# A hybrid mixer block: conditioning products one unit behind their loads, more taps in the xBC stage, one matmul for the context's high and low parts, pairwise squares at the front

## The chip, the cores and the metric

The kernel runs on one core of one Trainium2 chip. The metric is device time in microseconds of one execution, and lower is better.

## What is computed

One layer of a diffusion backbone over 512 latent tokens, with 256 context tokens as a prefix; the model width is 1024 and everything is fp32. Cut to what matters:

```python
mod_lat = split(silu(c) @ w_ada + b_ada, 6)         # conditioning: 6 x 1024 values for the latents
mod_ctx = split(silu(c_ctx) @ w_ada + b_ada, 6)     # of these the context needs the first two
h_ctx = modulate(rms_norm(ctx, norm1_g), mod_ctx[0], mod_ctx[1])
_, ctx_states = token_mixer(h_ctx, ...)             # the final SSD states of the context alone
h = modulate(rms_norm(x, norm1_g), mod_lat[0], mod_lat[1])

# token_mixer
z, xbc, dt, cv_in, pool_in, gate_logits = split(h @ w_in)
xbc = silu(depthwise_conv(xbc, 5 taps))             # latents and context
y = ssd_bidirectional(xbc, dt, ...)                 # chunked scans, both directions
y_ssd = rms_norm(y * silu(z)) @ ssd_w_out
y_conv = silu(layer_norm(depthwise_conv(a * sigmoid(b), 31 taps))) @ cv_w_out
y_pool = pool_mixer(pool_in)
merged = g0 * y_ssd + g1 * y_conv + g2 * y_pool     # sigmoid gates
x = x + mod_lat[2] * (merged @ w_out)

h = modulate(rms_norm(x, norm2_g), mod_lat[3], mod_lat[4])
x = x + mod_lat[5] * swiglu(h)
return rms_norm(x, final_g)
```

## The kernel before

Activations lie with 128 channels on the partitions and the tokens along the free axis: the 1024 channels of the latents are eight tiles of 128 x 512. A weight unit is 128 output channels by all inputs, 128 x 1024 values or 512 KB. To keep fp32 accuracy each operand is split into a high part, rounded to the format that TensorE takes in one pass, and a low part, the remainder. A product is then three matmuls into one PSUM bank (`mm3`, lines 132 to 137): high by high, high weight by low activation, low weight by high activation. `load_unit` (116) loads a unit into a raw buffer (`load_raw`, 111, three buffers named `wr`), ScalarE casts it to the high part `whi` (121) and VectorE subtracts to get the low part `wlo` (123). The context's activations `hc` are split the same way; the high and low part of one tile lie side by side, 256 columns each.

**Order of the work.** Instructions are written in program order; a planner then gives each engine a fixed order, by priorities and its own costs, and hands out the buffers of a name as they come free. `tc.high_priority` and `later(n)` move work forward and back in that order. `Ordered` (56) wraps the engines up to line 339: there each engine keeps the order of the source. Each engine, and the transfer queue of SyncE, then takes its work strictly in its fixed order.

**Front (176 to 338).** The first 2048 columns of the conditioning weights come in eight loads of 1 MB (`ada_load`), alternating with the tiles of x and the first three units of the input projection. `ada_mm(i)` multiplies one of them (16 small matmuls) and has ScalarE copy the result, `ada_out(i)` turns it onto the partitions with small matmuls, and VectorE adds the bias. An even i gives the scale of two channel tiles, the odd one behind it their shift. The mean square of x is an fp32 matmul with a matrix of 1/1024 (`mean`), which the trace shows as two matmuls; it reads `acc`, the sum of eight squares that ScalarE makes and VectorE adds (`sq_acc`). `rnorm` gives the reciprocal root. `h_scale` (VectorE) and `h_shift` (ScalarE and VectorE) make the high and low parts of the normalised input; `first(us, ks)` runs the matmuls of the units us for the tiles ks; `first_split` splits such a unit. `warm(n)` issues n matmuls whose result is not used. (In the trace all that goes through `Ordered` has line 62.)

**Input projection (350 to 741).** The convolution of 31 taps along rows (`conv31`) is 90 steps of two VectorE instructions each (line 403). `conv_steps(n)` releases n steps at a low priority; `CONV_STEPS_XBC` says how many in each of the twelve units of the xBC stage. In that stage (721 to 740) each unit is multiplied with the latents and, for the first ten, with the context; `conv5` runs five taps (669 on VectorE) and `xbc_tail` transposes on TensorE and builds the context's states.

**Scan, gates, convolution output (744 to 906).** The SSD scan of four chunks and two groups, woven with the units of z, of the two gates, and of the convolution output (`wcv`). What does not fit is written to HBM (`mrg`, `gat`, `zd`, `yd`).

**SSD output (927 to 942) and output projection (992 to 1025).** For each of eight tiles the SSD product is merged with `gat` and `mrg`, read back from HBM, and split; then the output projection `wout`, its first two tiles together, its last three in halves of the tokens.

**The other conditioning values.** The conditioning weights behind the first 2048 columns are 32 units, spread over the stages. `ada(n)` (854) loads n units of 512 KB into `wr` buffers and has VectorE multiply each with silu(c) and sum it along the free axis into one column of `mod_l` (line 861). It is called in `gate_tiles` (4 units), in the convolution output (4), in the SSD output (8), in the output projection (8) and in the down projection of the FFN (8).

**FFN (1028 to 1220).** Gate and up units, most of them by a scheme of seven half-size products (`fast_pair`), then the down projection.

Of the kernel before, what the change touches and what calls it, by code (L numbers as in the profile page):

```python
# [11 lines left out]
ALU = mybir.AluOpType  # L12
# [10 lines left out]
GATES_BEFORE_LN = 5  # L23
WOUT_HALVED = 3
CONV_STEPS_EARLY = (30, 18)
CONV_STEPS_XBC = (0, 0, 0, 1, 1, 1, 2, 2, 2, 2, 2, 2)
TAILS_KEPT_XBC = (1, 1, 1, 1, 1, 0, 0, 0, 0, 0, 0, 0)
I_CV, I_PL, I_XBC, I_Z, I_G1, I_G0 = 0, 12, 26, 38, 46, 54

# [23 lines left out]
def hybrid_block(ctx, tc, x, cx, cck, cc, wad, wada, vec, prm, cst, inv, win, wdt, wcv, wpl, wso, wout, wgu, wdn, out):  # L53
# [22 lines left out]
    def pt(pool, shape, tag, bufs, dt=F32):  # L76
        return pool.tile(shape, dt, tag=tag, name=nm(tag), bufs=bufs)
# [31 lines left out]
    lng_n, ssg_n, fin_n = neg[:, 0:6], neg[:, 6:14], neg[:, 14:22]  # L109

    def load_raw(src, n):
        raw = pt(per, [P, 1024], "wr", 3)
        nc.sync.dma_start(raw[:, :n], src)
        return raw

# [170 lines left out]
    ada_load(4)  # L286
    ada_out(0, sb)
    warm(14)
    acc = pt(per, [P, T], "sum", 1)
    for t in range(KT):  # L290
        sq_acc(acc, xs[t], t == 0, T)
    S.activation(junk, eps_t, AF.Abs_reciprocal_sqrt)
    first_split(0)
    sb = ada_mm(1)
    ada_load(5)
    first_load(2)
    ms = psp()
    PE.matmul(ms, mean, acc, start=True, stop=True)
    ada_out(1, sb)
    r = acc  # L300
    rnorm(ms, T, r)
    warm(4)
    h_scale(0, 1)
    sb = ada_mm(2)
    ada_load(6)
    ada_out(2, sb)
    h_shift(0, 1)
    warm(4)
    sb = ada_mm(3)
    ada_load(7)  # L310
    wdt_t = slot_c()[:, 0:256]
    nc.sync.dma_start(wdt_t, wdt)
    first((0,), (0, 1))
    h_scale(2, 3)
    ada_out(3, sb)
    first_split(1)
# [190 lines left out]
    def ctx_norm():  # L507
        x3 = xc[:, 0:2, :].rearrange("p a (t n) -> p (a t) n", n=TC)
        nc.sync.dma_start(x3, cx)
        xs_c = [x3[:, t, :] for t in range(KT)]  # L510
        r = norm_sum(xs_c, TC)
        hq = [slot_h([P, 4, 2, TC], F32R) for _ in range(2)]
        for t in range(KT):
            h = hq[t // 4][:, t % 4]
            make_h(xs_c[t], r, m1_c[:, t : t + 1], mod_c[:, t : t + 1], h[:, 0, :], h[:, 1, :])
            hc.append((h[:, 0, :], h[:, 1, :]))

    def pool_all():
        plp, waiting = [], []
# [201 lines left out]
    for q, i in enumerate((8, 9, 10, 11, 0, 1, 2, 3, 4, 5, 6, 7)):  # L721
        w = load_unit(win[I_XBC + q])
        o = mmp()
        for k in range(KT):
            mm3(o, w, k * P, hh[k], k == 0, k == KT - 1)
        pad = slot_c()
        nc.gpsimd.memset(pad[:, 0:2], 0.0)
        nc.gpsimd.memset(pad[:, 514:518], 0.0)
        S.copy(pad[:, 2:514], o)
        if i < 10:  # L730
            oc = mmp()
            for k in range(KT):
                mm3(oc[:, :TC], w, k * P, hc[k], k == 0, k == KT - 1)
            nc.gpsimd.memset(pad[:, 774:776], 0.0)
            S.copy(pad[:, 518:774], oc[:, :TC])
        conv_steps(CONV_STEPS_XBC[q], mark[-1])
        while len(tails) > TAILS_KEPT_XBC[q]:
            drain(tails.pop(0))
        tails.append(xbc_tail(i, pad))
        next(tails[-1], None)  # L740
# [110 lines left out]
    for i in range(24):  # L851
        adas.append(((2, 4, 3)[i // 8], i % 8))

    def ada(n=1):
        for _ in range(n):
            if not adas:
                return
            chunk, t = adas.popleft()
            raw = load_raw(wada[(chunk - 2) * 8 + t], 1024)
            i = chunk * 8 + t  # L860
            V.tensor_tensor_reduce(  # L861
                raw, raw, silb[0], 1.0, vc("b_ada", i), ALU.mult, ALU.add, mod_l[:, i : i + 1]
            )

    load_sil(f1.tile([P, 1024], F32, tag="sil1", name="sil1"))
    gens = [ssd_gen(0), ssd_gen(1)]
# [27 lines left out]
    with later(9000):  # L894
        for m in range(8):
            w = load_unit(wcv[m], 768)
            oc = mmp()
            for k in range(6):
                mm3(oc, w, k * P, cvy[k], k == 0, k == 5)
            sp = tmp()  # L900
            S.copy(sp, oc)
            nc.sync.dma_start(mrg[:, m, 1, :], sp)
            ada(m % 2)
    for z in range(4):
        for g in gens:
            next(g)
# [20 lines left out]
    for m in range(8):  # L927
        w = load_unit(wso[m])
        o = mmp()
        for k in range(KT):  # L930
            mm3(o, w, k * P, y_hl[k], k == 0, k == KT - 1)
        ga, mo = slot_a(), slot_c().rearrange("p (a b) -> p a b", b=T)
        nc.sync.dma_start(ga, gat[:, m])
        nc.sync.dma_start(mo, mrg[:, m])
        S.activation(ga, ga, AF.Sigmoid)
        V.tensor_tensor(mo[:, 1, :], mo[:, 1, :], ga[:, 1, :], ALU.mult)
        V.tensor_tensor(mo[:, 0, :], mo[:, 0, :], mo[:, 1, :], ALU.add)
        V.tensor_tensor(ga[:, 0, :], o, ga[:, 0, :], ALU.mult)
        V.tensor_tensor(mo[:, 0, :], mo[:, 0, :], ga[:, 0, :], ALU.add)
        mr = mo[:, 0, :]  # L940
        split(mg[m][0], mg[m][1], mr)
        ada(1)

    x1 = slot_x([P, KT, T])
    acc = pt(per, [P, T], "sum", 1)
# [72 lines left out]
    for sl in halves:  # L1018
        for m, (w, o) in zip(range(nh, 8), last):
            ms = rms_head(sl) if m == 7 else None  # L1020
            project(o, [(w, KT)], mg, sl)
            with tc.high_priority():
                residual(m, o, mod_l[:, 16 + m : 17 + m], xp[m // 2][:, m % 2, :], sl, slot_m(), ms)
            prescale(m, sl)
        h2_half(ms, sl)
    tc.keep_in_program_order(S.activation(junk, eps_t, AF.Silu))
    ph1.close()
# [171 lines left out]
    hid = hs  # L1199

    acc = pt(per, [P, T], "sum", 1)
    for m in range(8):
        ada(1)
        o = mmp()
# [129 lines left out]
```

## Time and profile before

| | |
|---|---|
| median of 3 runs | 977.23 us (976.6 to 978.72) |
| the profiled execution | 976.52 us, of it 974.7 us from its first to its last instruction |
| TensorE busy | 948.8 us (97%), 5420 matmuls |
| VectorE busy | 764.9 us (78%) |
| ScalarE busy | 492.2 us (50%) |
| transfers | 151.67 MB, mean 156 GB/s |
| granted TensorE clock, mean | 0.996 |

How to read it: the span is what the trace sees; the time is that of the whole execution. TensorE's matmuls overlap, so the duration of one is longer than the spacing between two. The granted clock is the share of TensorE's full clock that the chip allowed.

### The profile page before, as it was taken

What the parts mean: (1) busy time and instruction counts of PE and PEld (TensorE: products, weight loads), DVE (VectorE), ACT (ScalarE), POOL (GpSimd) and SP (SyncE); (2) the same over time, 40 slices, a digit from 0 to 9 for tenths busy, and PEclk for the clock granted to TensorE, in tenths of its full rate; (3) what the DMA queues carried; (4) which work ended last, traced back from release to release, by engine and by line L of the source; (5) the groups of instructions that cost most, each with busy time, mean ns of one, the idle gap of its engine ahead of it and who ended that gap; (6) DMA issues with size and microseconds to landing.
All of it is one profiled execution on the core that took longest, in us unless ns stands there. A gap on an engine that the chain in (4) does not pass through costs nothing.

```text
span 974.7 us, 14173 instructions
## 1 busy us (share of the span) xinstructions
PE 948.8 (97%) x5420; PEld 803.6 (82%) x5420; DVE 764.9 (78%) x1165; ACT 492.2 (50%) x815; POOL 15.9 (2%) x58
## 2 busy tenths in 40 slices
PE   6999999999999999999999989999999999999996
PEld 4678888888887776777888769989999999888885
DVE  5589999967889999987876976999889888643333
ACT  5683597335445254644844434745555556432331
POOL 0000000000000000000000000000000000000000
PEclk9999999999999999999999999999999999999998
DMA  9753455321112346665578984223232323343422
GB/s 364 282 187 110 164 179 173 109 87 65 67 65 76 108 162 195 216 205 196 176 259 318 363 278 170 91 104 131 101 117 87 119 99 122 127 141 109 136 79 87
DMA packets 55492, 151.67 MB, mean 156 GB/s; under 512 B 5760, under 2 KB 16512, under 8 KB 54272
## 3 DMA queue, kind: packets, MB, share of 16 engines
q1 hardware_dynamic: 55424, 150.77, 44.6%
q8 instruction: 42, 0.69, 0.3%
q14 instruction: 26, 0.21, 0.1%
HBM read 134.43 MB, written 16.32 MB: 155 GB/s over the span
## 4 chain that ended last, share of the span: by engine, by line
PE 86%; DVE 7%; DMA 4%; ACT 2%; issue 1%; SPq 0%; DVEq 0%; ACTq 0%
PE mm L137 19%; PE mm L135 19%; PE mm L136 19%; PE mm L1122 10%; PE ps L1122 8%; PE mm L62 1%; DMA C<-mrg 1%; DVE wlo L123 1%; DVE A L403 1%; PE ps L1039 1%; PE ps L763 1%; PE y L825 1%; PE ps L62 1%; PE ps L715 1%; DMA wr<-in_wso_dram 1%
## 5 line engine op out<-in xcount | busy, mean ns | idle before, releaser
L135 PE MATMUL mm<-hh,whi 128*128 128x512 f32 (+1 forms) x612 | 242.4, 396 | 0.0
L137 PE MATMUL mm<-hh,wlo 128*128 128x512 f32 (+1 forms) x612 | 241.2, 394 | 0.5 <-DVE wlo L123 0.5
L136 PE MATMUL mm<-hl,whi 128*128 128x512 f32 x576 | 228.9, 397 | 0.0
L121 ACT CAST whi<-wr 128x1024 fp32r<-128x1024 f32 (+1 forms) x115 | 116.9, 1019 | 212.1 <-PE mm L136 167.4
L123 DVE TENSOR_TENSOR wlo<-wr,whi 128x1024 fp32r<-128x1024 f32 (+1 forms) x112 | 132.2, 1183 | 63.1 <-ACT whi L121 62.0
L137 PEld LDWEIGHTS mm<-hh,wlo 128*128 128x128 f32 x612 | 115.0, 188 | 28.3 <-issue 2.8
L135 PEld LDWEIGHTS mm<-hh,whi 128*128 128x128 f32 x612 | 115.1, 188 | 26.0 <-issue 1.7
L136 PEld LDWEIGHTS mm<-hl,whi 128*128 128x128 f32 x576 | 108.3, 188 | 25.0 <-issue 2.7
L403 DVE SCALAR_TENSOR_TENSOR A<-U,vec_t,A 128x504 f32<-128x504 f32 (+14 forms) x180 | 115.4, 684 | 0.1
L129 ACT CAST shi<-S 128x1024 fp32r<-128x1024 f32 x36 | 37.9, 1052 | 32.1 <-DVE S L1110 26.3
L1122 PE MATMUL mm<-T,shi 128*128 128x256 f32 x288 | 53.5, 283 | 0.0
L669 DVE SCALAR_TENSOR_TENSOR C<-C,vec_t,C 128x772 f32<-128x772 f32 (+1 forms) x48 | 46.9, 977 | 4.9 <-ACT C L667 2.4
L130 DVE TENSOR_TENSOR slo<-S,shi 128x1024 fp32r<-128x1024 f32 x36 | 44.1, 1225 | 5.8 <-ACT shi L129 5.7
L818 ACT ACTIVATE E<-E,sbias 128x128 f32<-128x128 f32 x128 | 40.0, 392 | 10.6 <-DMA E<-cumd 10.5
L1122 PEld LDWEIGHTS mm<-T,shi 128*128 128x128 f32 x288 | 44.8, 191 | 0.0
L129 ACT CAST whi<-wr 128x1024 fp32r<-128x1024 f32 (+1 forms) x36 | 30.0, 835 | 26.0 <-PE ps L1122 21.4
L861 DVE CUSTOM_DVE_ANT_0 wr<-wr,sil,vec_t 128x1024 f32<-128x1024 f32 x24 | 30.8, 1282 | 13.4 <-DMA wr<-in_wada_dram 13.4
L137 PE MATMUL mm<-H,wlo 128*128 128x256 f32 (+1 forms) x124 | 38.0, 307 | 2.9 <-DVE wlo L123 2.8
L1122 PE MATMUL mm<-T,slo 128*128 128x256 f32 x144 | 40.8, 284 | 0.0
L130 DVE TENSOR_TENSOR wlo<-wr,whi 128x1024 fp32r<-128x1024 f32 (+1 forms) x36 | 34.5, 958 | 7.6 <-ACT whi L129 6.0
L135 PE MATMUL mm<-H,whi 128*128 128x256 f32 (+1 forms) x124 | 37.8, 305 | 0.0
L136 PE MATMUL mm<-H,whi 128*128 128x256 f32 (+1 forms) x124 | 37.7, 304 | 0.0
(383 smaller groups left out, 2039.4 us busy)
## 6 DMA issues: line engine op xcount, KB each, us to landing
wr<-in_win_dram SPq DMA_DIRECT2D x62, 512.0 KB, 3.7
wr<-in_wgu_dram SPq DMA_DIRECT2D x44, 512.0 KB, 3.4
wr<-in_wada_dram SPq DMA_DIRECT2D x32, 512.0 KB, 4.0
E<-cumd SPq DMA_DIRECT2D x16, 512.0 KB, 5.3
wr<-in_wdn_dram SPq DMA_DIRECT2D x16, 512.0 KB, 3.9
X<-in_wad_dram SPq DMA_DIRECT2D x4, 1024.0 KB, 10.6
H<-in_wad_dram SPq DMA_DIRECT2D x4, 1024.0 KB, 11.2
mrg<-tmp SPq DMA_DIRECT2D x16, 256.0 KB, 4.0
```

Source lines behind the costliest of these rows:

```text
L121: S.copy(hi[:, :n], raw[:, :n])
L123: V.tensor_tensor(lo[:, :n], raw[:, :n], hi[:, :n], ALU.subtract)
L129: S.copy(dst_hi, src)
L130: V.tensor_tensor(dst_lo, src, dst_hi, ALU.subtract)
L135: PE.matmul(o, hi[:, col : col + P], rh, start=first, stop=False)
L136: PE.matmul(o, hi[:, col : col + P], rl, start=False, stop=False)
L137: PE.matmul(o, lo[:, col : col + P], rh, start=False, stop=last)
L403: V.scalar_tensor_tensor(accs[e][:, :, o], ins[e][:, :, q], vc("dw_w", (2 * j + e) * 31 + 15 + d), accs[e][:, :, o], ALU.mult, ALU.add)
L669: tap = V.scalar_tensor_tensor(a[:, 0:n], pad[:, k : n + k], vc("conv_w", i * 5 + k), a[:, 0:n], ALU.mult, ALU.add)
L818: S.activation(dec[d][:, j, :], dec[d][:, j, :], AF.Identity, bias=sbias[:, z, c : c + 1])
L861: V.tensor_tensor_reduce(raw, raw, silb[0], 1.0, vc("b_ada", i), ALU.mult, ALU.add, mod_l[:, i : i + 1])
L1122: PE.matmul(o[:, left], x[:, cs], rhs[k][y], start=first and k + n == 0, stop=k == 3 and n == 2, skip_group_check=True,)
```

## The change

- *Front.* The eight squares are added in four pairs; the four sums go through the averaging matrix one after the other, into one PSUM bank, three ahead of `ada_mm(1)` and the last behind it. `h_shift(0, 1)` moves ahead of `ada_mm(2)`, one `warm(4)` goes, and `first((0,), (0, 1))` moves ahead of `ada_mm(3)`.
- *xBC.* `CONV_STEPS_XBC` grows from 15 steps to 24. The context's high weight part meets the high and low activation parts in one matmul of 512 columns, whose two halves VectorE adds afterwards.
- *Conditioning.* `ada` now loads a unit and multiplies the one loaded before it (`ada_product`, `ada_rest`). The convolution output takes 5 units in place of 4, the SSD output 7 in place of 8, and the down projection issues its first load ahead of its loop. There are four raw buffers in place of three.

```diff
--- before.py
+++ after.py
@@ -23,7 +23,7 @@
 GATES_BEFORE_LN = 5
 WOUT_HALVED = 3
 CONV_STEPS_EARLY = (30, 18)
-CONV_STEPS_XBC = (0, 0, 0, 1, 1, 1, 2, 2, 2, 2, 2, 2)
+CONV_STEPS_XBC = (1, 1, 1, 2, 2, 2, 3, 3, 3, 2, 2, 2)
 TAILS_KEPT_XBC = (1, 1, 1, 1, 1, 0, 0, 0, 0, 0, 0, 0)
 I_CV, I_PL, I_XBC, I_Z, I_G1, I_G0 = 0, 12, 26, 38, 46, 54
 
@@ -109,7 +109,7 @@
     lng_n, ssg_n, fin_n = neg[:, 0:6], neg[:, 6:14], neg[:, 14:22]
 
     def load_raw(src, n):
-        raw = pt(per, [P, 1024], "wr", 3)
+        raw = pt(per, [P, 1024], "wr", 4)
         nc.sync.dma_start(raw[:, :n], src)
         return raw
 
@@ -286,31 +286,37 @@
     ada_load(4)
     ada_out(0, sb)
     warm(14)
-    acc = pt(per, [P, T], "sum", 1)
+    sq = []
     for t in range(KT):
-        sq_acc(acc, xs[t], t == 0, T)
+        q = slot_c()[:, :T] if t % 2 == 0 else tmp()
+        S.activation(q, xs[t], AF.Square)
+        if t % 2:
+            V.tensor_tensor(sq[-1], sq[-1], q, ALU.add)
+        else:
+            sq.append(q)
     S.activation(junk, eps_t, AF.Abs_reciprocal_sqrt)
     first_split(0)
+    ms = psp()
+    for q in sq[:3]:
+        PE.matmul(ms, mean, q, start=q is sq[0], stop=False)
     sb = ada_mm(1)
+    PE.matmul(ms, mean, sq[3], start=False, stop=True)
     ada_load(5)
     first_load(2)
-    ms = psp()
-    PE.matmul(ms, mean, acc, start=True, stop=True)
     ada_out(1, sb)
-    r = acc
+    r = pt(per, [P, T], "sum", 1)
     rnorm(ms, T, r)
     warm(4)
     h_scale(0, 1)
+    h_shift(0, 1)
     sb = ada_mm(2)
     ada_load(6)
     ada_out(2, sb)
-    h_shift(0, 1)
-    warm(4)
+    first((0,), (0, 1))
     sb = ada_mm(3)
     ada_load(7)
     wdt_t = slot_c()[:, 0:256]
     nc.sync.dma_start(wdt_t, wdt)
-    first((0,), (0, 1))
     h_scale(2, 3)
     ada_out(3, sb)
     first_split(1)
@@ -513,7 +519,7 @@
         for t in range(KT):
             h = hq[t // 4][:, t % 4]
             make_h(xs_c[t], r, m1_c[:, t : t + 1], mod_c[:, t : t + 1], h[:, 0, :], h[:, 1, :])
-            hc.append((h[:, 0, :], h[:, 1, :]))
+            hc.append((h[:, 0, :], h.rearrange("p a n -> p (a n)")))
 
     def pool_all():
         plp, waiting = [], []
@@ -730,9 +736,12 @@
         if i < 10:
             oc = mmp()
             for k in range(KT):
-                mm3(oc[:, :TC], w, k * P, hc[k], k == 0, k == KT - 1)
+                ks = slice(k * P, k * P + P)
+                PE.matmul(oc, w[0][:, ks], hc[k][1], start=k == 0, stop=False, skip_group_check=True)
+                PE.matmul(oc[:, :TC], w[1][:, ks], hc[k][0], start=False, stop=k == KT - 1, skip_group_check=True)
             nc.gpsimd.memset(pad[:, 774:776], 0.0)
             S.copy(pad[:, 518:774], oc[:, :TC])
+            V.tensor_tensor(pad[:, 518:774], oc[:, TC:], pad[:, 518:774], ALU.add)
         conv_steps(CONV_STEPS_XBC[q], mark[-1])
         while len(tails) > TAILS_KEPT_XBC[q]:
             drain(tails.pop(0))
@@ -851,16 +860,24 @@
     for i in range(24):
         adas.append(((2, 4, 3)[i // 8], i % 8))
 
+    loaded = deque()
+
+    def ada_product():
+        i, raw = loaded.popleft()
+        V.tensor_tensor_reduce(raw, raw, silb[0], 1.0, vc("b_ada", i), ALU.mult, ALU.add, mod_l[:, i : i + 1])
+
     def ada(n=1):
         for _ in range(n):
-            if not adas:
-                return
-            chunk, t = adas.popleft()
-            raw = load_raw(wada[(chunk - 2) * 8 + t], 1024)
-            i = chunk * 8 + t
-            V.tensor_tensor_reduce(
-                raw, raw, silb[0], 1.0, vc("b_ada", i), ALU.mult, ALU.add, mod_l[:, i : i + 1]
-            )
+            if adas:
+                chunk, t = adas.popleft()
+                loaded.append((chunk * 8 + t, load_raw(wada[(chunk - 2) * 8 + t], 1024)))
+            if len(loaded) > 1 or not adas:
+                ada_rest(1)
+
+    def ada_rest(n=99):
+        while loaded and n:
+            ada_product()
+            n -= 1
 
     load_sil(f1.tile([P, 1024], F32, tag="sil1", name="sil1"))
     gens = [ssd_gen(0), ssd_gen(1)]
@@ -900,7 +917,7 @@
             sp = tmp()
             S.copy(sp, oc)
             nc.sync.dma_start(mrg[:, m, 1, :], sp)
-            ada(m % 2)
+            ada(m in (0, 2, 4, 6, 7))
     for z in range(4):
         for g in gens:
             next(g)
@@ -939,7 +956,10 @@
         V.tensor_tensor(mo[:, 0, :], mo[:, 0, :], ga[:, 0, :], ALU.add)
         mr = mo[:, 0, :]
         split(mg[m][0], mg[m][1], mr)
-        ada(1)
+        if m < 7:
+            ada(1)
+        else:
+            ada_rest()
 
     x1 = slot_x([P, KT, T])
     acc = pt(per, [P, T], "sum", 1)
@@ -1022,6 +1042,7 @@
             with tc.high_priority():
                 residual(m, o, mod_l[:, 16 + m : 17 + m], xp[m // 2][:, m % 2, :], sl, slot_m(), ms)
             prescale(m, sl)
+            ada_rest()
         h2_half(ms, sl)
     tc.keep_in_program_order(S.activation(junk, eps_t, AF.Silu))
     ph1.close()
@@ -1199,6 +1220,7 @@
     hid = hs
 
     acc = pt(per, [P, T], "sum", 1)
+    ada(1)
     for m in range(8):
         ada(1)
         o = mmp()
```

## Rows read from the trace of the kernel before

**Rows 1.** Stages: us, busy of PE PEld DVE ACT POOL, PEclk, DMA share, GB/s

```profile
0.00:23.00 23.00, 14.66 (x122) 10.73 (x122) 11.86 (x31) 11.48 (x19) 0.20 (x4) 1.00 0.93 360
23.00:48.30 25.30, 24.19 (x161) 17.43 (x157) 14.51 (x33) 15.81 (x26) 1.31 (x5) 1.00 0.74 294
48.30:200.00 151.70, 151.70 (x697) 121.93 (x697) 141.58 (x230) 93.01 (x168) 2.47 (x13) 1.00 0.45 152
...
312.00:460.00 148.00, 145.56 (x696) 106.57 (x695) 134.48 (x219) 72.59 (x151) 10.18 (x8) 1.00 0.54 177
...
517.00:592.00 75.00, 71.52 (x301) 56.77 (x300) 60.49 (x88) 32.06 (x38) 0.00 (x0) 0.98 0.89 320
...
652.00:950.00 298.00, 297.86 (x2030) 276.87 (x2030) 209.74 (x288) 140.52 (x220) 0.00 (x0) 1.00 0.34 114
```

**Rows 2.** Timeline of VectorE and ScalarE, front: start, us, what, [idle before]

```profile
11.05 5.47 DVE L62 TENSOR_TENSOR sum<-sum,tmp 128x512 f32<-128x512 f32 x7
...
20.11 0.37 ACT L62 COPY M<-ps 128x256 f32<-128x256 f32 x1 [1.68 <-PE ps L62]
...
21.43 1.39 ACT L62 ACTIVATE hh<-W,mod_l 128x512 fp32r<-128x512 f32 x2 [0.95 <-DVE W L62]
```

**Rows 3.** Timeline of TensorE, front.

```profile
15.26 1.07 PE L62 MATMUL ps<-H,cct 128*32 128x256 f32 x16
16.57 1.13 PE L62 MATMUL ps<-sum,mean 128*128 128x512 f32 x2 [0.24 <-DVE junk L663]
...
20.53 0.61 PE L62 MATMUL ps<-cck_t,M 128*128 128x2 f32 x4 [0.49 <-ACT M L62]
21.00 1.14 PE L62 MATMUL y<-mean 128*128 128x128 f32 x8
...
23.07 0.51 PE L62 MATMUL mm<-hh,whi 128*128 128x512 f32 x1
...
25.95 1.07 PE L62 MATMUL ps<-X,cct 128*32 128x256 f32 x16 [0.86 <-DMA X<-in_wad_dram]
```

**Rows 4.** The chain that ended last, 345 to 356 us: start, us, what.

```profile
349.96 0.23 PE mm L135
...
350.87 0.86 PE ps L798 x2
```

**Rows 5.** The page's transfer issues: count, KB each, us to landing.

```profile
H<-in_wad_dram SPq DMA_DIRECT2D x4, 1024.0 KB, 11.2
```

**Rows 6.** Busy time in xBC: one context part (tile H, without POOL), one unit.

```profile
258.87:261.74 2.87, 2.87 (x24) 2.82 (x23) 0.00 (x0) 0.00 (x0) 1.00 0.00 0
...
258.87:268.90 10.03, 10.03 (x64) 8.85 (x62) 8.21 (x12) 4.43 (x8) 0.17 (x3) 1.00 0.14 55
```

**Rows 7.** VectorE's groups, 200 to 312 us: busy us, mean ns, idle before.

```profile
L706 DVE TENSOR_TENSOR W<-ps,wdec 128x256 f32<-128x256 f32 x15 | 6.2, 420 | 9.0 <-PE ps L703 9.0
```

**Rows 8.** The page's costliest groups.

```profile
L403 DVE SCALAR_TENSOR_TENSOR A<-U,vec_t,A 128x504 f32<-128x504 f32 (+14 forms) x180 | 115.4, 684 | 0.1
```

**Rows 9.** Timeline of TensorE, 370 to 374 us.

```profile
373.42 1.12 PE L763 MATMUL ps<-W,btok 128*128 128x512 f32 x2 [1.59 <-DVE W L761]
```

**Rows 10.** VectorE's waits, 500 to 592 us: total us, times, longest.

```profile
DVE wr L861 <- DMA wr<-in_wada_dram: 10.8, 8, 3.4
```

**Rows 11.** Timeline of the transfer queue, 549 to 571 us.

```profile
551.90 0.33 SPq L113 DMA_DIRECT2D wr<-in_wada_dram  x1
...
555.51 2.06 SPq L113 DMA_DIRECT2D wr<-in_wout_dram  x2
```

**Rows 12.** Timeline of VectorE and TensorE, 562 to 580 us.

```profile
564.11 1.22 DVE L123 TENSOR_TENSOR wlo<-wr,whi 128x1024 fp32r<-128x1024 f32 x1
...
565.38 0.50 PE L137 MATMUL mm<-H,wlo 128*128 128x512 f32 x1 [1.96 <-DVE wlo L123]
...
578.99 0.50 PE L137 MATMUL mm<-H,wlo 128*128 128x512 f32 x1 [0.84 <-DVE wlo L123]
```

**Rows 13.** Busy time in the stretch behind the stand at 563 us.

```profile
566.63:570.04 3.41, 3.41 (x9) 2.63 (x8) 2.83 (x4) 0.67 (x1) 0.00 (x0) 0.50 0.73 275
```

## Prediction

> **What bounds the kernel now.** I read the page first, then the busy times by stage, then the chain of waits and TensorE's own waits, then the timelines around each of these. TensorE is busy in nearly every stage from its first to its last us [rows 1], so no other engine bounds the whole, and an edit pays only where TensorE stands still, runs at half clock, or has work taken away. From 652 to 950 us TensorE lacks 0.1 us, so the part of the change in the down projection (one product of a conditioning unit ahead of the loop) can give nothing. What is left lies in three places: the front (8.3 us idle in the first 23, and 1.1 up to 48.3), the scan stage (2.4 us between 312 and 460), and the stage from the SSD output projection to the first output tiles (3.5 us between 517 and 592, plus a spell at half clock). The profiled execution took 976.52 us; the sum below is made against it. The median of the three runs shown is 977.23, and 0.2% of that, 2 us, is about what a measurement here can tell from no change: faster means below 975.3, slower above 979.2.
>
> **The front.** Before, VectorE adds the eight squares in a row, 5.47 us for seven additions, 0.78 each [rows 2]; TensorE meanwhile ends its warm-up matmuls, does the second conditioning product from 15.26 and waits until 16.57 for the sum [rows 3]. After, four additions are left, so VectorE is up to 2.3 us earlier. But the sum over pairs goes to TensorE: four fp32 matmuls of 512 columns with the averaging matrix in place of one, and three of them stand in TensorE's order ahead of the second conditioning product. Such a matmul issues for 0.86 us (a pair of passes) [rows 4]. So from 15.26: three take 2.6 (17.85), the product 1.07 (18.9), and only then comes the fourth, where the old one came at 16.57: the norm is 2.35 us later. TensorE, not VectorE, sets this point now.
>
> Next the order. The shifts of the first two tiles (ScalarE, two in 1.39 us from 21.43) now stand ahead of the copy of conditioning product 2; before, that copy ran at 20.11, ahead of them [rows 2]. After: shifts from 23.8 to 25.2, the copy 0.37 behind them, then on TensorE the four small transposing matmuls of that product (0.5, as from 20.53 to 21.00), then the first weight matmul, near 26.1; it was at 23.07 [rows 3]. That is 3.0 late. TensorE, done with product 2 near 22.4 (18.9 + 0.86 + 0.5 + 1.1 of warm-up + 1.07), stands some 3 us ahead of it. Conditioning product 3 (1.07) was done ahead of the first weight matmuls; now it comes behind them, and its copy is waited for directly. So the scale and shift of tiles 2 and 3, which hang on it, are 4.4 late. The old order had then waited 0.86 for a transfer at 25.95 [rows 3]; that wait drops out, but beside it the shifts of these tiles were being made, so I credit only 0.2 and put the front at **+4.2**. After it the old TensorE runs almost without a pause: of the 1.1 us idle between 23 and 48.3 [rows 1] 0.86 is that transfer. Nothing absorbs the delay, and the stage after it has no idle time either, so it is carried to the end. Bounds: +1.5 if only the later norm counts and the transfer's wait swallows the rest; +5.9 if the new stand of 3 us brings TensorE's clock down, at the price of the spell near 566 (below). The warm-up matmuls that are removed filled a pause and cost nothing. The queue of transfers is saturated here (share 0.93 [rows 1]) and deep, 11.2 us from issue to landing [rows 5], so loads issued 3 to 5 us later land no later.
>
> **The xBC stage.** One context unit before: 24 matmuls of 256 columns in 2.87 us, 0.12 each [rows 6]. After: 8 of 512 columns at 0.23 [rows 4] and 8 of 256: 1.84 + 0.96 = 2.80. Ten units save **0.6** in all. The column count is the same; only the cost beside the columns is saved. The Trainium skill, TensorE: Matmul & The Clock Gate, "Back-to-back issue gap", gives columns over 2.4 GHz plus 2.5 ns for an isolated matmul; by it, as an estimate, a unit falls from 2.62 to 2.60 and the ten save 0.2. The trace's 0.120 differs from that page's 0.109, so the row decides. VectorE gets an addition that reads PSUM, 256 columns, 0.42 as in [rows 7], ten times, and nine more steps of two taps at 0.68 [rows 8], 12 us of taps that leave the scan stage. A unit lasts 10.03 us with VectorE busy 8.2 [rows 6]; where a third step is added: 8.2 + 1.4 + 0.4 = 10.0, just full, in three units out of twelve, and 8.6 in the last three. In the stage before, 48 to 200 us, VectorE was busy 141.6 of 151.7 us and TensorE never stood [rows 1]. I take no cost; bound: +2 if the weight remainders come behind taps.
>
> **The scan stage.** The longest stand of TensorE is at 373.42, 1.59 us behind a VectorE multiplication [rows 9]. With 12 us less of taps VectorE reaches it earlier. I take **-1.6**; bounds 0 (the planner fills the room with other low-priority work) and -2.4, all idle time of the stage.
>
> **Conditioning products one unit behind, a fourth buffer.** VectorE takes its work in order, and from 500 to 592 it stood 10.8 us in front of products whose weights had not landed [rows 10]. Behind it are queued the weight remainders that TensorE waits for. The transfer queue suffers too: a weight load that needs a buffer goes out only when such a product is done. In [rows 11] a conditioning load at 551.90 goes ahead of the two output-projection loads from 555.51; the remainder of the first is made only at 564.11, behind the merge of the last SSD tile, and TensorE stands 1.96 us, to 565.38 [rows 12]. Then it runs at half clock: 9 matmuls in 3.41 us [rows 13], where 15 would go at 0.23; 6 or 7 lost are about 1.6 us. At 578.99 it stands 0.84 more for the next remainder [rows 12]. After, one unit moves out of the SSD projection into the convolution projection, where the queue has room; no conditioning load is left ahead of the output-projection loads, and products take data that landed long ago. Without the load of 551.90 the next ones land 1.4 us earlier (512 KB at the 360 GB/s of the saturated front [rows 1]), and they no longer wait for buffers that a product frees: the remainder then fits ahead of the merge. I take 2.0 + 1.6 + 0.8 = **-4.4**. Bounds: -5 with the small stands beside it, and 0: a product held back also holds its buffer, so the fourth buffer may only pay for that.
>
> Sum: 976.5 + 4.2 - 0.6 - 1.6 - 4.4 = 974.1.
>
> **Rivals.** (1) *The weights of the output projection stay late*: queue and VectorE keep their order, only part of the stand goes. For it: the share of the queue in this stage is 0.89 [rows 1], and the bytes are the same. Against it: the chain from product to load is plain in the rows. With 1 to 2 us back there and 0 to 1.6 in the scan: 976.5 + 4.2 - 0.6 - 1.5 - 0.8 = 977.8, no change. (2) *The front decides, slower*: TensorE's pause of 3 us ahead of the first weight matmul brings the clock to 0.5 as the stand of 2 us at 563 did [rows 12, 13]; against it, that of 1.6 at 373 did not (clock 1.00 in the scan stage [rows 1]). Front +5.9, output stage -1, xBC -0.6: 980.8. It decides from the point at which the other stages give back less than 1.5. The Trainium skill, same page, "What's actually happening", calls the slow clock the default that activity lifts; the spell at 566 agrees, and the new pause speaks by that rule for this rival. (3) *The front is free*: the transfers, not TensorE's order, set its end. For it the share of 0.93; against it the 1.07 and 0.86 us matmuls stacked on one path. Then +1.5: 976.5 + 1.5 - 6.6 = 971.4. (4) *xBC fills VectorE over the brim* and TensorE waits for weight remainders: +2 there, 976.1; for it the 10.0 of 10.0, against it the stage from 48 to 200.
>
> **Numbers.** Forecast 0.37 (972 to 975.3 around it); rival 3: 0.10; rivals 1 and 4: 0.33 together; rival 2: 0.20. Faster 0.47, same 0.33, slower 0.20. Predicted 974.1. Range 970.0 to 980.0: it leaves out about one in ten on each side. The forecast's own range is 972 to 975.3.
>
> **What would show it.** Right: the first weight matmul near 26 instead of 23.07, TensorE idle ahead of it, the tiles of the front ending near 52.5 instead of 48.3; no stand near 563 + 4 and no half clock behind it; VectorE near full between 250 and 290; no waits for the conditioning loads. Wrong: a front that ends where it did, a stand that only moves from one output tile to the next, or new stands in xBC.

## The result, and the profile after

The changed kernel takes 985.61 us (median of 4 runs, 983.46 to 987.24), the kernel before beside it 977.59: a ratio of 1.008, with the 95% interval 1.0058 to 1.0103 (so in brackets below). It is slower by about 8 us, and the forecast of 974.1 with its range of 970 to 980 is wrong. The profiled execution took 985.93 us, its span is 983.9 us.

The busy times by stage, of the kernel after, in the columns of [rows 1]; the stages are shifted to where they now begin:

```profile
0.00:27.42 27.42, 16.41 (x105) 11.60 (x105) 10.37 (x25) 12.19 (x21) 0.20 (x4) 0.97 0.93 361
27.42:32.00 4.58, 4.58 (x23) 2.40 (x23) 1.94 (x6) 0.36 (x1) 0.00 (x0) 0.50 0.69 290
32.00:56.15 24.15, 22.95 (x154) 16.30 (x151) 12.46 (x29) 14.67 (x24) 1.31 (x5) 0.98 0.56 207
319.60:467.60 148.00, 145.05 (x694) 106.18 (x694) 125.25 (x204) 73.06 (x151) 9.63 (x8) 1.00 0.56 180
524.90:599.90 75.00, 70.33 (x293) 55.41 (x292) 60.16 (x87) 32.18 (x38) 0.00 (x0) 0.98 0.90 326
```

The front now ends at 56.15 us instead of 48.30, so 7.85 us are lost there in the two profiled executions, and 4.6 us of it run at half clock (0.50 in the second row), which they did not before. Of the 7.85 us, 1.07 are not the change's: the warm-up matmuls, the same code in both kernels, ended at 16.33 us instead of 15.26 [rows 3]. In eleven other profiled kernels with the old front they ended between 15.32 and 16.84, and from there the old front lasted 32.70 to 33.23 us (33.04 in the kernel before). In the scan stage TensorE still stands idle for 3 us out of 148, in the output stage for 4.7 out of 75: the two places that were to give time back [rows 1] are no better.

TensorE's timeline of the front after:

```profile
16.33 2.74 PE L62 MATMUL ps<-C,mean 128*128 128x512 f32 x6
19.00 1.07 PE L62 MATMUL ps<-H,cct 128*32 128x256 f32 x16
20.00 1.12 PE L62 MATMUL ps<-C,mean 128*128 128x512 f32 x2
...
22.39 1.07 PE L62 MATMUL ps<-X,cct 128*32 128x256 f32 x16
26.55 1.01 PE L62 MATMUL ps<-cck_t,M 128*128 128x2 f32 x4 [3.08 <-ACT M L62]
27.42 0.77 PE L62 MATMUL mm<-hh,whi 128*128 128x512 f32 x1
...
30.26 1.94 PE L62 MATMUL ps<-H,cct 128*32 128x256 f32 x16
```

Three averaging matmuls (six in the trace, 2.7 us) stand ahead of the second conditioning product, the fourth behind it at 20.00, where the sum went in at 16.57 [rows 3]. Behind conditioning product 2 TensorE stands idle for 3.08 us (a stand, below) until ScalarE's copy is done, and the first weight matmul comes at 27.42 instead of 23.07. From there to 32 us the clock is 0.50, and the third conditioning product takes 1.94 instead of 1.07.

The stage from the SSD output projection to the halves of the output projection (its last three tiles), first of the kernel before, then of the kernel after:

```profile
517.61:602.94 85.33, 81.85 (x374) 66.39 (x373) 67.05 (x97) 38.75 (x48) 0.00 (x0) 0.98 0.86 308
```

```profile
524.93:611.91 86.98, 82.31 (x374) 66.43 (x372) 66.54 (x96) 38.20 (x48) 0.00 (x0) 0.98 0.83 299
```

It is 1.65 us longer. VectorE's wait for conditioning weights, which was 10.8 us in eight waits [rows 10], is 14.1 us in six (the waits of VectorE, 507 to 602 us). In the chain that ended last such a load, 6.94 us under way, leads to a product:

```profile
DVE wr L867 <- DMA wr<-in_wada_dram: 14.1, 6, 3.3
```

```profile
555.44 6.94 DMA wr<-in_wada_dram
562.40 1.29 DVE wr L867
```

The stand of TensorE at 565.38, 1.96 us with half clock behind it [rows 12, 13], has shrunk to one of 0.52 us at 572.78 with the clock at 1.00. The same pattern comes 19.5 us later, at 592.25, as the timeline of VectorE, that of TensorE, and the busy times of the stretch behind the stand show:

```profile
589.76 1.28 DVE L867 CUSTOM_DVE_ANT_0 wr<-wr,sil,vec_t 128x1024 f32<-128x1024 f32 x1 [2.07 <-DMA wr<-in_wada_dram]
...
590.97 1.22 DVE L123 TENSOR_TENSOR wlo<-wr,whi 128x1024 fp32r<-128x1024 f32 x1
```

```profile
592.25 0.53 PE L137 MATMUL mm<-H,wlo 128*128 128x512 f32 x1 [2.50 <-DVE wlo L123]
```

```profile
592.30:596.30 4.00, 4.00 (x11) 3.12 (x12) 4.00 (x5) 3.21 (x4) 0.00 (x0) 0.57 0.93 336
```

A conditioning product waits 2.07 us for its load, the weight remainder behind it in VectorE's order comes late, TensorE stands 2.50 us and then runs at a clock of 0.57. A product one unit behind still meets a load that has not landed.

The output projection's first two weight loads did not go out earlier either, though no conditioning load stands ahead of them now. In SyncE's queue the load of two tiles of x stands there, and it waited 5.1 us for VectorE to end a merge that frees its buffer (1.5 us before). Of the kernel after, SyncE's waits and its queue:

```profile
SPq L996 <- DVE C L956: 5.1, 1, 5.1
```

```profile
565.05 0.33 SPq L996 DMA_DIRECT2D A<-in_x_dram  x1
565.43 0.90 SPq L113 DMA_DIRECT2D wr<-in_wout_dram  x2
```

That is 40.5 us into the stage, against 37.9 before (555.51 [rows 11]).

Over the whole span, by the first matmul of each stage, the kernel after is late by 7.85 us at the end of the front, 7.6 at the first scan step (313.68 before, 321.28 after), 7.3 at the SSD output projection and 9.0 at the halves; the span is 9.2 us longer.

### The profile page after: what moved, and what is told of

Same layout as the page of the kernel before. It is cut to its first block, busy times and chain, and to the rows that moved or that the text cites. A ratio compares the mean times of both kernels' runs of the same rounds, so it can differ in the third digit from the quotient of the medians.

```text
span 983.9 us, 14008 instructions
## 1 busy us (share of the span) xinstructions
PE 953.4 (97%) x5338; PEld 801.1 (81%) x5338; DVE 763.6 (78%) x1172; ACT 495.5 (50%) x815; POOL 15.3 (2%) x58
## 4 chain that ended last, share of the span: by engine, by line
PE 86%; DVE 6%; DMA 5%; ACT 1%; issue 1%; SPq 0%; DVEq 0%; ACTq 0%
PE mm L137 17%; PE mm L135 17%; PE mm L136 17%; PE mm L1143 10%; PE ps L1143 8%; PE mm L62 2%; PE mm L740 2%; PE ps L62 2%; DMA wr<-in_wada_dram 1%; DMA A<-gat 1%; DMA E<-cumd 1%; PE ps L1060 1%; PE ps L772 1%; PE mm L741 1%; DVE A L409 1%
## 5 line engine op out<-in xcount | busy, mean ns | idle before, releaser
L740 PE MATMUL mm<-H,whi 128*128 128x512 f32 x80 | 28.6, 397 | 0.0
L1143 PEld LDWEIGHTS mm<-T,slo 128*128 128x128 f32 x144 | 27.5, 191 | 0.0
L1143 PE MATMUL ps<-T,shi 128*128 128x256 f32 x144 | 26.8, 283 | 0.1
```

The costliest lines, as they stand in the source:

```text
L740: PE.matmul(oc, w[0][:, ks], hc[k][1], start=k == 0, stop=False, skip_group_check=True)
L1143: PE.matmul(o[:, left], x[:, cs], rhs[k][y], start=first and k + n == 0, stop=k == 3 and n == 2, skip_group_check=True,)
```

## The experiments

Theory after the result: (A) the front is the loss, by the averaging matmuls and the order of the prediction plus half clock; (B) in the output stage the transfers themselves are too many for the time, so what is done to the products only moves the stands. Rivals: the xBC stage or the fourth buffer costs something; or it is VectorE's order there, and the edit only missed it.

**One part at a time.** Each is the kernel before with one hunk of the change: the front, the conditioning products, the xBC stage, the buffers.

```diff
-        raw = pt(per, [P, 1024], "wr", 3)
+        raw = pt(per, [P, 1024], "wr", 4)
```

> The kernel before with the new front alone. Theory (the front makes the whole loss: order on TensorE and ScalarE, then half clock): slower by 7 to 8.5 us, the first token-wide matmul behind the front (48.3 before) near 55.5 to 56.5. Rival (the front costs the 4.2 us of the prediction and the rest of the loss comes from the other parts): slower by 3.5 to 5 us. If the start of this one profiled execution was merely late, the time is 6 to 7 us longer and the front ends near 55.

> The kernel before with the conditioning products one unit behind their loads, the moved units and the fourth raw buffer. Prediction: 4.4 us faster, no stand at 563 us. Theory after the result (the stand only moves from the first output tile to a later one, since the loads themselves go out late): within 2 us of the kernel before, VectorE still waiting some 35 us for conditioning loads, with stands of TensorE of 1 to 3 us between 550 and 595.

> The kernel before with the taps moved into the xBC stage and the fused context matmuls. Prediction: 2.2 us faster (0.6 of matmuls, 1.6 in the scan). Theory after the result: 0.3 to 0.6 us faster, the stand at 371 us moved, not gone. Rival: VectorE full in xBC, 1 to 2 us slower.

> The kernel before with four raw buffers instead of three and nothing else. If late weight loads for want of a buffer make the stands between 550 and 585 us: 3 to 5 us faster. If the queue's bytes make them: within 1 us of the kernel before.

The front alone: 984.89 us, ratio 1.0062 (1.0039 to 1.0086). Conditioning (with its fourth buffer) 978.53, 0.9998 (0.9986 to 1.001); xBC 978.56, 1.0003 (0.999 to 1.0017); four buffers alone 977.48, 0.9992 (0.9975 to 1.0009). So the front is the loss, 6.3 us of the 8.0 (the two intervals overlap), and the three others give nothing that can be measured. The 6.3 us lie below the 7 to 8.5 of the theory and above the 3.5 to 5 of its rival; they are the 6 to 7 that were expected if the profiled execution of the kernel after had merely started late, as its warm-up did; the front's end was then to be near 55, but came at 52.82 in the one execution profiled. In the profiled execution of the front alone (981.44 us) the same stand of TensorE is there, but the clock holds, as TensorE's timeline and the busy times behind it show:

```profile
15.56 2.74 PE L62 MATMUL ps<-C,mean 128*128 128x512 f32 x6
...
25.78 0.61 PE L62 MATMUL ps<-cck_t,M 128*128 128x2 f32 x4 [3.08 <-ACT M L62]
26.25 0.48 PE L62 MATMUL mm<-hh,whi 128*128 128x512 f32 x1
```

```profile
26.25:32.00 5.75, 4.75 (x45) 2.56 (x44) 3.86 (x11) 3.62 (x7) 0.00 (x0) 1.00 0.96 377
```

That end is 4.52 us late:

```profile
52.82 1.05 PE L272 MATMUL ps<-W,C 128*32 128x512 f32 x2
```

The six executions fall apart by their mean granted clock: two at 0.995 took 981.4 and 981.9 us, four at 0.989 to 0.992 took 984.5 to 987.9. Only the first of them was profiled; where the clock was low in those four no trace shows.

In the conditioning part alone the output projection's first weights went out at 558.54, not at 555.51 as before [rows 11], with four conditioning loads right behind them (SyncE's queue):

```profile
558.54 0.90 SPq L113 DMA_DIRECT2D wr<-in_wout_dram  x2
559.49 9.40 SPq L113 DMA_DIRECT2D wr<-in_wada_dram  x4
```

**The front, order and pause.** The first has only the moves (the squares are added as before), the second the whole new front with 14 warm-up matmuls put into TensorE's pause.

```diff
+    h_shift(0, 1)
     sb = ada_mm(2)
...
-    h_shift(0, 1)
-    warm(4)
+    first((0,), (0, 1))
     sb = ada_mm(3)
...
-    first((0,), (0, 1))
```

```diff
     sb = ada_mm(2)
     ada_load(6)
+    warm(14)
     ada_out(2, sb)
```

> The new order of the front alone (shifts ahead of product 2, the first weight matmuls ahead of product 3, one warm-up less), with the squares summed on VectorE and averaged in one matmul as before. Theory: the four averaging matmuls cost 2.35 of the 4.2, so this is 1.5 to 2.5 us slower where the clock holds, and up to 5 where it falls, since TensorE stands here as long. Rival (the averaging matmuls are the whole cost): no change.

> The new front alone on the kernel before, with 14 more unused matmuls on TensorE between conditioning product 2 and its transposing matmuls, where the new order lets TensorE stand some 3.4 us. They depend on nothing and end before the copy that TensorE waits for. Theory (the order costs 4.2 to 4.5 us, and the fall of the clock behind the stand, in some executions, the rest): 4 to 5 us slower than before, no half clock between 20 and 40 us, and less spread than the front alone, which ran from 981.4 to 987.9. Rival (the clock has no part, later transfers make the rest): as the front alone, 6 us slower, same spread.

The moves alone: 983.59 us, 1.005 (1.0033 to 1.0066), 5.5 us slower, where 1.5 to 2.5 were expected with the clock held and up to 5 without. The new front with the pause filled: 982.7, 1.0048 (1.0026 to 1.0071), which does not stand apart from the front alone; it lies in the 4 to 5 us that were expected. The moves alone already bring the half clock, in the busy times of the stretch behind the stand:

```profile
23.80:30.60 6.80, 5.65 (x26) 3.27 (x26) 3.26 (x8) 2.32 (x5) 0.00 (x0) 0.50 0.96 401
```

**Fewer bytes in the output stage.** The kernel before, with the eight conditioning units of the SSD output projection moved into the xBC stage, products directly behind their loads and three buffers as before; in the second, twelve.

```diff
+        ada(q >= 4)
         conv_steps(CONV_STEPS_XBC[q], mark[-1])
...
-        ada(1)
+        ada(0)
```

> The kernel before, with the eight conditioning units of the SSD projection loaded and multiplied in the xBC stage instead (one in each of its last eight units); products directly behind their loads, three raw buffers. Theory (the bytes of the conditioning loads fill the transfer queue from 517 to 565 us, so weights land late whatever the order): the stands from 545 to 570 us go, 2.5 to 4.5 us faster, queue share there from 0.95 to 0.75. Rival (VectorE's order makes the stands, not the bytes): within 1.5 us of before.

> As the eight units moved, but twelve: one in each xBC unit, none in the SSD projection, four instead of eight in the output projection. Theory (bytes): as with eight, and the stands from 575 to 590 us go too, 4 to 6 us faster. Rival: VectorE, 8.2 busy of 10 us in the xBC units, gets 1.3 more in each and makes TensorE wait there; within 1.5 us of before.

Eight units: 970.96 us, 0.9923 (0.9908 to 0.9938), faster than both kernels, and by 7.1 us where 2.5 to 4.5 were expected. Busy times of it from 517 us on:

```profile
517.00:565.00 48.00, 48.00 (x212) 39.35 (x211) 35.16 (x50) 22.09 (x25) 0.00 (x0) 1.00 0.85 291
565.00:592.00 27.00, 27.00 (x128) 22.50 (x127) 21.63 (x29) 13.81 (x19) 0.00 (x0) 1.00 0.84 287
```

The units went where the queue had room, as the busy times of the xBC stage show, of the kernel before and of this one (share 0.19 and 0.33):

```profile
200.00:312.00 112.00, 112.00 (x660) 97.70 (x659) 87.91 (x112) 54.17 (x84) 1.72 (x28) 1.00 0.19 66
```

```profile
200.00:312.00 112.00, 112.00 (x659) 97.64 (x658) 97.56 (x129) 52.82 (x82) 1.70 (x28) 1.00 0.33 108
```

In the output stage TensorE does not stand any more and the clock is 1.00 throughout; the transfers' share from 517 to 565, 0.94 before, is 0.85, and the two output-projection loads go out at 546.60 instead of 555.51, now ahead of the load of x. Twelve units: 974.89, 0.9961 (0.9948 to 0.9975), 3.2 us faster where 4 to 6 were expected. There is no stand in the output stage either, but the xBC stage does not hold four more: TensorE stands there for a copy of ScalarE, and half clock follows (timeline and busy times):

```profile
245.24 1.11 PE L699 MATMUL ps<-ident,C 128*128 128x128 f32 x4 [2.63 <-ACT C L695]
```

```profile
244.70:248.20 3.50, 2.96 (x11) 2.67 (x12) 3.47 (x6) 3.21 (x5) 0.00 (x0) 0.51 0.36 114
```

**Waits or bytes?** Moving eight units takes away the waits and the bytes together. The next kernels part them: the 16 products of the output stage multiply other data, so that VectorE does the same work without waiting, with the loads issued (no_wait) or left out (no_bytes). These kernels leave out the conditioning values of the 16 units; they serve for the time alone.

```diff
+            if loose[0]:
+                raw = pt(per, [P, 1024], "scr", 1)
+                load_raw(wada[(chunk - 2) * 8 + t], 1024)
+                V.tensor_tensor_reduce(
+                    raw, silb[0], silb[0], 1.0, vc("b_ada", i), ALU.mult, ALU.add, mod_l[:, i : i + 1]
+                )
+                continue
```

> The kernel before, but in the SSD output and the output projection the 16 conditioning products multiply silu(c) with itself, so VectorE does the same work and waits for no load; the 16 loads are still issued, and their data is left unused (these conditioning values are not computed). Theory, the bytes: the queue still carries 8 MB there, the weights of the output projection land as late, and the time stays within 2 us of before, 976 to 980, with TensorE's stands of 2 to 4 us between 517 and 592. Rival, the waits of VectorE's order, as the prediction had it: the stands go, 970 to 973.

> The same with the 16 loads left out as well (8 MB less in the queue). Theory, the bytes: no stands between 517 and 592 and no half clock there, 969 to 972, as with eight units moved away. Rival, the waits: the same time as without waits alone, within 1.5 us. If this one stays near 977, the stands come from neither, and the cause is in the weights' own way.

Both expectations missed: 989.59 us, 1.0116 (1.0101 to 1.0131), and 986.03, 1.0084 (1.0067 to 1.01). With no late input the planner put all 16 products, 20.4 us of VectorE, into the scan stage, and the scan's last matmul (line 825) came at 461.1 and 462.3 us instead of 450.6. Only their output stage can be read: 82.73 us and 78.69 us. The pair was made again with the products held in place, by multiplying the weight remainder that VectorE has just made:

```diff
-        ada(1)
+        ada(1, w[1].bitcast(F32))
```

> As no_wait, but each of the 16 products multiplies the low part of the weight unit being used, which VectorE itself made a little earlier: it stays in its place, does the same work and waits for no load. The 16 loads are issued and their data is unused (these conditioning values are not computed). Theory, the bytes: the stage from the SSD output projection to the halves stays above 82 us (85.4 before, 78.8 with eight units moved away), the time at 974 to 979. Rival, the waits in VectorE's order: the stage falls to 79, the time to 970 to 972.

> As no_wait2, with the 16 loads left out as well. Theory, the bytes: the stage falls to 79 us, no stands, 969 to 972. Rival, the waits: within 1 us of no_wait2.

Without waits: 974.71 us, 0.9969 (0.9956 to 0.9982). Without waits and bytes: 970.56, 0.9922 (0.9907 to 0.9937). Their output stage, in busy times:

```profile
517.10:599.83 82.73, 80.55 (x375) 66.92 (x373) 66.79 (x97) 38.04 (x48) 0.00 (x0) 0.98 0.83 312
```

```profile
517.85:596.52 78.67, 78.67 (x374) 65.84 (x372) 65.74 (x97) 37.91 (x48) 0.00 (x0) 1.00 0.65 228
```

VectorE's busy time is alike in both (66.79 and 65.74). Of the 6.7 us between this stage before (85.33) and without both, taking all waits away gives 2.6 and taking the 8 MB away 4.1. What is left without waits is one stand with half clock behind it, for a remainder that VectorE made at 562.60 behind a merge:

```profile
563.87 0.50 PE L137 MATMUL mm<-H,wlo 128*128 128x512 f32 x1 [2.18 <-DVE wlo L123]
```

With the bytes gone the planner sends the output projection's weights much earlier (the first at 537.31 instead of 552.62), ahead of the loads of x, and puts that remainder ahead of the merge. So "the bytes" means what the loads take of the queue, the buffers and the plan together; the buffers alone (wr4) are not it. No kernel has the bytes gone and the order of the other loads kept, so the share of each is not shown.

**Only the two late loads.** Bytes, waits and products as before, but the output projection's first two weight units are loaded ahead of the last SSD tile's merge:

```diff
+        if m == 7:
+            pre = [load_unit(wout[0]), load_unit(wout[1])]
         ga, mo = slot_a(), ...
```

> The kernel before with the first two weight units of the output projection loaded ahead of the merge of the last SSD tile, and so ahead of that tile's conditioning load; bytes, products and waits are the same. Theory, the bytes: the stand of 2 us near 563 goes, but the next units come late instead; the stage from 517.6 to the halves, 85.3 us before, falls to 83 to 85.5, the time to 975 to 978. Rival, only the place of the two loads counts, as the prediction had it: the stand, the half clock behind it and with them 3.5 us go, the stage takes 81 to 82, the time is 973 to 974.5.

978.88 us, 1.0007 (0.9996 to 1.0017): no change, a little above the 975 to 978 of the theory and far from the 973 to 974.5 of its rival. The stand at 565 is gone, and one of 4.17 us has come 13 us later, for the next unit's weights, as TensorE's timeline and the busy times show:

```profile
578.26 0.80 PE L135 MATMUL mm<-H,whi 128*128 128x512 f32 x1 [4.17 <-ACT whi L121]
```

```profile
518.13:604.77 86.64, 81.91 (x374) 67.11 (x372) 66.94 (x98) 38.58 (x48) 0.00 (x0) 0.96 0.87 303
```

**The other parts on the better kernel.** With the output stage quiet, the parts were put on the kernel with eight units moved (970.96 us): the new front, the same with the pause filled, the pair squares alone in the old order, and the context's matmuls of 512 columns alone.

```diff
     first_split(0)
+    ms = psp()
+    for q in sq[:3]:
+        PE.matmul(ms, mean, q, start=q is sq[0], stop=False)
     sb = ada_mm(1)
+    PE.matmul(ms, mean, sq[3], start=False, stop=True)
```

> The kernel with eight conditioning units moved into xBC (971.0, spread 0.6), plus the new front. Since that kernel is quiet behind the front, its spread is that of the front. Theory: 975.2 to 975.8 in executions where the clock holds, 977 to 979.5 where it falls to half behind TensorE's stand, so a spread of 2 to 4 us. Rival (the clock has no part; the spread of the front alone was that of the stage at 550 us): one value near 975.5 with a spread below 1 us.

> The same with 14 unused matmuls in TensorE's stand. Theory: all executions 975.2 to 976, as the clock has no pause to fall behind. Rival (no part of the clock): the same median as without them, within 0.5 us.

> The quiet kernel with the squares added in pairs and averaged in four matmuls on TensorE, the rest of the front in the old order. Theory: the norm comes 2.35 us later, 973.0 to 973.6. Rival (the transfers of the front hide it, which ends the front at 34 to 37 us): 971.0 to 971.8.

> The quiet kernel with the context's high and low parts in one matmul and ten additions on VectorE. Prediction: 0.6 us faster, 970.4. Rival (VectorE, full in xBC with the eight products, makes TensorE wait): 0.5 to 3 us slower.

Measured, to the kernel before: new front 977.83, 0.9989 (0.9973 to 1.0005); pause filled 974.97, 0.9978 (0.9961 to 0.9994); pair squares alone 973.76, 0.9956 (0.994 to 0.9972); context matmuls alone 969.84, 0.9916 (0.9894 to 0.9938), the best of all, though not apart from the 970.96 without them. The new front alone and the last two came out near what was expected; the filled pause did not, which was to bring all executions to 975.2 to 976. The new front without and with the filled pause, in busy times of the same stretch:

```profile
25.33:32.15 6.82, 5.64 (x26) 3.27 (x26) 3.27 (x8) 2.34 (x5) 0.00 (x0) 0.50 0.70 292
```

```profile
25.33:32.15 6.82, 5.57 (x52) 3.40 (x52) 4.94 (x12) 4.47 (x9) 0.00 (x0) 1.00 1.01 406
```

The clock is 0.50 in the one and 1.00 in the other; the front ends at 55.77 and at 52.55, which is 39.80 and 37.26 us behind the end of the warm-up (15.97 and 15.29). The ten executions with the filled pause split again by mean clock: six at 0.996 and 0.997 took 974.0 to 975.1 us, four at 0.994 took 977.4 to 979.7. Without the filling one in ten was at 0.997 (it took 973.97), the others at 0.991 to 0.994. So the low mean clock seems rarer with the pause filled, but the intervals of the two kernels overlap. Where the clock fell in those four no trace shows, and it need not be in this pause: one of the ten executions with the pair squares alone, which leave the old order and make no such pause, was at 0.994 too (977.52 us).

## Why the prediction was wrong, by its steps

**The front, +4.2: the mechanism right, the choice of the clock wrong.** The steps came out where the clock held. Counted from the end of the warm-up matmuls, so that their own spread drops out, the front lasted 33.04 us before (15.26 to 48.30 [rows 1, 3]) and 37.26 in the front alone (15.56 to 52.82): 4.22 more. In its parts: the fourth averaging matmul is 3.67 us behind the warm-up's end (16.33 to 20.00), where the one before came 1.31 behind it [rows 3], 2.36 later; the pair squares alone put the front's end 2.66 later (35.39 against 32.73 us behind the warm-up, in the two profiled executions with eight units moved) and cost 2.8 us in the medians (973.76 against 970.96, with 978.29 and 978.07 for the kernel before beside them). The moves alone lasted 37.13 us (17.11 to 54.24) with half clock; less the 2.56 that it costs (below), an estimate, they add 1.5 to 1.9. The new order adds a stand of 3.08 us where 3 were expected, the first weight matmul came at 26.25 in the front alone (near 26 was predicted), and the front's end at 52.82 (52.5). Nothing absorbed it. What failed is the choice of the clock: it was taken as held, at +4.2, with +5.9 as the bound where it falls. It fell in the profiled executions of the changed kernel, of the moves alone and of the new front with eight units moved; by the mean clock, in four of six executions of the front alone and in nine of ten with eight units moved. So the changed kernel's 7.85 us are 4.22 of averaging and order, 2.56 of half clock (39.82 us behind the warm-up, 16.33 to 56.15, against 37.26), and the 1.07 of a warm-up that ended late. Of the 2.56, 0.40 are the transposing matmuls (1.01 against 0.61), the rest the weight matmuls and products behind them. The bound took the price, 1.7, from the spell near 566, where 6 or 7 matmuls were lost; here the half clock also took the conditioning product (1.94 against 1.07) that the scale and shift of the next tiles hang on. Rival 2 was right in direction, and too cheap.

The Trainium skill, TensorE: Matmul & The Clock Gate, "What's actually happening", calls the slow clock the default that activity lifts. The rows with clock 0.50 behind the stands agree; but the same stand of 3.08 us left it at 1.00 in the front alone, so that rule did not say which of the two an execution gets.

**Conditioning, -4.4: the step that failed.** It said that the products take data that landed long ago, that the output projection's first loads go out 1.4 us earlier, and that stand, half clock and small stands go. The remainder for the first output tile did come ahead of the last merge, as predicted, and its stand shrank to 0.52. But the two loads went out 2.6 us later in the stage, behind a load of x that waited 5.1 us for a merge; that wait was not in the prediction. And 20 us on a product met a load that had gone out only 5.8 us before it (583.99, the product at 589.76): a stand of 2.50 and a half clock came at 592, and the stage grew by 1.65 us. The prediction took a chain of two loads and one product, read at one place, for the bound of a stage whose queue is nearly full (0.89 [rows 1]). The pair of kernels without waits shows that VectorE's waits were worth 2.6 us at most; 4.1 hang on the loads and the plan that goes with them, and moving the two late loads only moves the stand. This was rival 1, whose 1 to 2 us back were still too many: the edit alone measured 0, its interval reaching from -1.4 to +1.0 us.

**Scan, -1.6: failed.** The stand at 373.42 [rows 9] is only moved: with the xBC part alone TensorE stands for 0.94 us at 422.86 and for 1.55 here (timeline):

```profile
409.69 1.10 PE L766 MATMUL ps<-W,btok 128*128 128x512 f32 x2 [1.55 <-DVE W L764]
```

VectorE's busy time in the scan fell (134.48 [rows 1] to 125.25 of 148 us in the kernel after), and TensorE's idle time did not (2.4 to 3.0). Only the bound 0 was right. Why VectorE, with less to do, still comes late there is left open.

**xBC, -0.6 and no cost: right in kind, about half in size.** A context part lasts 2.82 us after, where 2.80 was expected and 2.87 measured before [rows 6]; in the changed kernel (busy times):

```profile
208.97:211.79 2.82, 2.82 (x18) 2.44 (x16) 0.00 (x0) 0.59 (x1) 0.00 (x0) 1.00 0.06 20
```

From the first context part to the first scan step the stage gained 0.26 us (112.57 to 112.31), too little for the medians to show. Rival 4, VectorE over the brim, did not come: TensorE was busy for all of that stage.

**The sum with the measured terms**, front, xBC, scan with convolution output, and output stage: 976.5 + 7.85 - 0.2 - 0.3 + 1.65 = 985.5, and the profiled execution took 985.93. Of the 11.4 us between this sum and the forecast, 6.05 are the conditioning step, 3.65 the front (half clock and late warm-up, less than 0.1 in its order), 1.3 the scan and 0.4 xBC.

## What to carry to other kernels

When a stage's transfer queue is nearly full, reordering the work that waits for it moves the stand from one tile to the next; look at every load that stands ahead of the late one in the queue, and at what each waits for. What paid here was to take the loads out of the stage, into one whose queue has room; count what the engines there still hold, as twelve units showed. A pause of TensorE at the front can cost more than its own length: here 2.6 us of half clock came on top where the clock fell, so price that as well, above all where a chain of small dependent products follows. Moving additions from a half idle VectorE to TensorE by four fp32 matmuls costs the time that they take there (2.4 to 2.7 us here), when TensorE sets the path. Before two profiled executions are set beside each other at a late point, take out what had already differed ahead of the change.

## What the runs showed of the hardware

A stand of TensorE of the same length, 3.08 us by the trace, in the same front, was followed by a clock of 0.50 in two kernels' profiled executions (the kernel after, and the new front with eight units moved) and of 1.00 in a third (the front alone). With the new front and eight units moved, with the pause filled or not, executions at a mean clock of 0.996 and 0.997 took 974.0 to 975.1 us, those at 0.991 to 0.994 took 975.2 to 979.7. Shorter stands were followed by half clock too: 2.5 us at 592 in the kernel after, 2.6 at 245 with twelve units moved, 1.96 at 565 in the kernel before [rows 12, 13]; one of 1.80 us at 585.58 with the conditioning part alone was not (1.00 from 585.6 to 589.6). What decides between the two is left open.
